# A two-layer hybrid trunk on one core: attention with a different vector split and transposed outputs, an fp32 staggered block preparation, and a delta rule dealt in half steps

## The chip, the core and the metric

The kernel runs on one core of a Trainium2 chip. The core has TensorE (PE in the rows: matmuls, with their weight loads listed apart as PEld), VectorE (DVE), ScalarE (ACT) and GpSimd (POOL), and SyncE (SP), which here does nothing but issue DMAs. Every DMA of this kernel, plain or transposing, is issued by SP, one after the other in program order. The metric is the device time of one execution in microseconds.

## What is computed

Two layers run over 1024 latent tokens and 128 context tokens of width 1024. In each layer three groups of heads read the same normalized input, and their outputs are concatenated, projected and added to the stream:

```python
q = _rope_2d(aq...); k = _rope_2d(ak...)                       # A: attention, 8 query heads, 2 kv heads
o_a = _latent_attention(q, k, v, k_ctx, v_ctx, sink) * silu(ag)   # window of +-128 tokens, plus the context
o_b = _sgu(bu, bv, ...) * silu(bg)                             # B: gated mixing inside 128-token chunks
q_c, k_c, v_c, g, beta = _gdn_features(...)                    # C: gated delta rule, 4 heads, 64-token chunks
a_mat = where(strict, einsum(kb, k) * decay, 0)                # per chunk
t_mat = triangular_solve(a_mat + eye, eye)
def step(state, ...):                                          # chunk after chunk, in both directions
    v_new = u - w @ state
    o     = q_dec @ state + a_qk @ v_new
    state = state * exp(g_last) + k_dec.T @ v_new
x = x + gate * rmsnorm(concat(o_a, o_b, o_c * silu(cg)) @ w_out)
```

## The kernel before, in words

**Tiling.** The tokens are nine tiles of 128: eight latent ones and the context tile, `CTX` = 8. Most operands of matmuls are kept as two f16 halves, a high part and the rest, so that a product takes three f16 matmuls; the delta rule's small 64x64 products are in fp32.

**Two strands in a layer.** `chain()` is the delta rule: the features, then `scan`. `fill()` is everything else that needs the input only: branch B, the gates, and `attention`. `merge` deals them out: the chain yields an estimated cost after each piece, and as much of the fill is emitted as that cost times `FILL` = 0.9 pays for; the tile scheduler then orders each engine's queue by that order of writing. `out_layer` follows alone.

**`scan`.** Ten blocks are prepared first, two of the context and eight of the first pair of heads (about 213 to 302 us of the span in layer 0, 925 to 1005 in layer 1), then comes a triangular solve (`lat_solve`), then `steps(0)`, the 18 steps of the state recurrence for the first pair of heads. The eight blocks of the second pair are prepared inside `steps(0)`, one in every second step. Then a second solve and `steps(1)`. In time: `steps(0)` 380 to 515 and 1080 to 1205 us, `steps(1)` 570 to 690 and 1275 to 1400 us.

**Preparing a block (`prep`, L429).** GpSimd forms the log-decay masks `gt` (L433). The features q and k are fp32; ScalarE, GpSimd and VectorE make f16 halves of them in `PK` (L438 to L443). TensorE transposes the eight pieces (L447) into the PSUM bank of `psw`, ScalarE copies them to `PT` (L449), TensorE forms the products k k and k q (L454) in the same bank's next use, and the sums of the log decays (L459, L460) in the bank of `psv`. ScalarE takes the exponential, `E` (L462), GpSimd multiplies it by beta (L463), VectorE multiplies the products by `E` into `NA` (L465). `psw` and `psv` have one buffer each, and `steps` uses the same two.

**A step of the recurrence (`steps`, L535).** GpSimd scales q and k (`qk` L546, `kd` L548). `pre` turns the scaled q (L556) and forms w (L559) in `psw`. `post` forms v_new (L572, L573) in `psv`, VectorE copies it to `vn` (L575), then come the state's increment (L577), the output (L580, L581) and the new state `S` (L583, L585). The whole of a step is written before the fill gets its turn.

**Attention.** `attention`'s `prep` projects a tile, loads its rotary table `rt` (L889), applies it in `rope_tile` (two multiplies, two half adds: L849 to L854), and turns the f16 halves `ql` into `qT` by a transposing DMA (`turn`, L899). K tiles go the same way first (`rt` at L998). `heads` forms the scores (L921, L922), VectorE adds the mask and takes the maximum (L926), ScalarE makes two exponentials (L928, L929), GpSimd the low half (L931), a transposing DMA makes `PT` (L933). Up to six heads later `weigh` multiplies by V (L947): per key block one matmul of 128 columns (the high half of P with both halves of V) and one of 64 columns. After four heads `normal` forms the denominator (`es` L957, `den` L960 and L961, `rd` L963), scales the gate (L964), adds the two 64-column parts (ScalarE copy L969, VectorE L970) and multiplies (L971). One tile later `finish` transposes the result on TensorE (L977), splits it into f16 halves `OTA` (ScalarE L980, VectorE L981) and writes it to `mix_d` in HBM (L982). `out_layer` reads `mix_d` back.

## Time and profile before

| | us |
|---|---|
| median of 3 runs | 1485.67 (1478.66 to 1486.11) |
| the profiled execution | 1488.63 |
| its span | 1486.8 |
| PE busy, PEld busy | 1312.4 (88%), 1008.0 (68%) |
| DVE busy | 957.6 (64%) |
| ACT busy | 656.4 (44%) |
| POOL busy | 649.5 (44%) |

A busy share is an average over all stages. A windows row gives the same sums for one stretch, with the TensorE clock that was granted there as a part of full speed and the mean busy share of the DMA engines. A groups row puts together all instructions of one line, engine and shape: how many, their summed busy time, the mean duration of one, and the idle time of the engine just before them with what ended it. A matmul's mean duration overlaps with its neighbours', so that the busy time divided by the count is nearer to what one costs in a row of them. A waits row gives how long an engine stood at that line for that releaser, how often, and the longest.

### The profile page before, as it was taken

The numbers are of one execution on the slowest core, as the hardware profiler recorded it, in microseconds if no ns is written. First come the engines' busy times: TensorE is split into PE (matmuls) and PEld (weight loads), VectorE is DVE, ScalarE is ACT, GpSimd is POOL, SyncE is SP. The second block draws the span as 40 slices with busy tenths as digits, with TensorE's granted clock in tenths as the row PEclk, the third lists the DMA queues.
The fourth block names the chain that finished last, engine by engine and source line by source line (L and its number), as shares of the span: only waits on it lengthen the run. The fifth ranks groups of instructions, "written<-read, shape, count | busy, mean of one in ns | idle before, by whom it ended". The sixth has DMA issues, their size and how long they took to land.

```text
span 1486.8 us, 37911 instructions
## 1 busy us (share of the span) xinstructions
PE 1312.4 (88%) x15191; PEld 1008.0 (68%) x15191; DVE 957.6 (64%) x2302; ACT 656.4 (44%) x1483; POOL 649.5 (44%) x890
## 2 busy tenths in 40 slices
PE   6899988799989599979997998879998769997997
PEld 2665566476667487767886655668777658876786
DVE  2865689985565576563547676889586466677333
ACT  2733545523665415642334345442377322665211
POOL 0751246534565325662223433541578514577200
PEclk9999999899999889989998998998899779999999
DMA  9331035727963217683432211332177211677553
GB/s 361 108 84 41 23 98 129 171 74 166 206 165 90 42 52 140 109 228 89 145 113 74 53 36 58 97 71 64 34 134 152 54 39 39 138 122 140 163 177 107
DMA packets 301562, 162.90 MB, mean 110 GB/s; under 512 B 212622, under 2 KB 277938, under 8 KB 301386
## 3 DMA queue, kind: packets, MB, share of 16 engines
q1 hardware_dynamic: 301261, 160.45, 43.8%
q8 instruction: 119, 1.95, 0.6%
q14 instruction: 57, 0.47, 0.1%
q10 hardware_dynamic: 125, 0.04, 0.0%
HBM read 95.78 MB, written 24.28 MB: 81 GB/s over the span
## 4 chain that ended last, share of the span: by engine, by line
PE 42%; DVE 20%; DMA 14%; POOL 10%; issue 9%; ACT 5%; SPq 1%; ACTq 0%; DVEq 0%; POOLq 0%
PE ps L170 11%; PE ps L1052 9%; PE ps L312 6%; DMA PT<-P 4%; DMA mix_d<-oc 3%; DVE sv L502 2%; POOL P L931 2%; DVE sv L500 2%; PE ps L698 2%; PE ps L947 1%; DVE y L319 1%; PE ps L249 1%; DMA wm<-in_w_mod_dram 1%; POOL gt L433 1%; DVE sS L926 1%
## 5 line engine op out<-in xcount | busy, mean ns | idle before, releaser
L170 PEld LDWEIGHTS <-X 128*128 128x128 f16 x3888 | 352.9, 101 | 110.5 <-issue 42.5
L170 PE MATMUL ps<-wg,X 128*128 128x256 f16 x2592 | 331.5, 281 | 11.8 <-DVE wg L161 4.5
L1052 PEld LDWEIGHTS <-OTm 128*128 128x128 f16 x1728 | 169.3, 99 | 24.5 <-DMA OTm<-mix_d 2.5
L931 POOL TENSOR_TENSOR P<-sS,P 128x512 f16<-128x512 f32 (+2 forms) x144 | 152.1, 1060 | 77.1 <-ACT sS L929 75.4
L1052 PE MATMUL ps<-wo,OTm 128*128 128x256 f16 x1296 | 151.0, 276 | 2.1 <-DMA OTm<-mix_d 2.1
L312 PE MATMUL ps<-X,wg 128*128 128x512 f16 (+1 forms) x864 | 146.2, 328 | 1.8 <-ACT wg L160 1.4
L926 DVE CUSTOM_DVE_ANT_0 sS<-ps,am,nsk 128x512 f32<-128x512 f32 (+2 forms) x144 | 95.0, 671 | 52.6 <-POOL P L931 27.7
L928 ACT ACTIVATE P<-sS,nmx 128x512 f16<-128x512 f32 (+2 forms) x144 | 93.6, 660 | 64.2 <-DVE nmx L926 61.9
L170 PE MATMUL ps<-wb,X 128*128 128x256 f16 x864 | 107.9, 289 | 15.2 <-ACT wb L160 13.8
L312 PEld LDWEIGHTS <-wg 128*128 128x128 f16 x864 | 74.0, 99 | 69.1 <-ACT wg L160 1.8
L145 POOL TENSOR_TENSOR rs<-ms,mhalf 128x1 f32<-128x1 f32 x36 | 21.1, 589 | 175.9 <-DVE ms L1061 108.8
L929 ACT ACTIVATE sS<-sS,nmx 128x512 f32<-128x512 f32 (+2 forms) x144 | 94.8, 659 | 3.3
L947 PE MATMUL ps<-Vt,PT 128*128 128x128 f16 (+1 forms) x992 | 69.6, 211 | 26.8 <-DMA PT<-P 23.6
L319 DVE SCALAR_TENSOR_TENSOR y<-zT,cw,y 128x1156 f32<-128x1156 f32 x48 | 68.9, 1439 | 27.5 <-ACT y L317 26.9
L947 PEld LDWEIGHTS <-PT 128*128 128x128 f16 x992 | 51.6, 100 | 45.3 <-DMA PT<-P 30.8
L502 DVE TENSOR_TENSOR sv<-sv 128x31 f32<-128x31 f32 (+15 forms) x186 | 75.0, 403 | 4.3
L500 DVE TENSOR_TENSOR sv<-sv 128x31 f32<-128x31 f32 (+15 forms) x186 | 72.6, 391 | 4.2
L922 PE MATMUL ps<-KT,qT 128*128 128x128 f16 (+2 forms) x272 | 70.1, 273 | 0.0
L921 PE MATMUL ps<-KT,qT 128*128 128x128 f16 (+2 forms) x272 | 61.5, 274 | 8.4 <-DVE nmx L926 6.6
L835 POOL TENSOR_TENSOR th<-th,M 128x256 f32<-128x256 f32 (+1 forms) x20 | 13.5, 679 | 126.4 <-DVE th L834 97.5
L1055 ACT ACTIVATE sq<-ps 128x512 f32<-128x512 f32 x36 | 21.4, 595 | 102.1 <-PE ps L1052 59.1
L288 DVE TENSOR_SCALAR hf<-ps,AB 128x128 f32<-128x128 f32 x117 | 39.7, 402 | 38.9 <-PE ps L281 38.7
(271 smaller groups left out, 2866.8 us busy)
## 6 DMA issues: line engine op xcount, KB each, us to landing
st<-in_w_in_dram SPq DMA_DIRECT2D x40, 512.0 KB
st<-in_w_mod_dram SPq DMA_DIRECT2D x32, 512.0 KB
OTm<-mix_d SPq DMA_DIRECT2D x18, 512.0 KB
wm<-in_w_mod_dram SPq DMA_DIRECT2D x16, 512.0 KB
xt<-in_x_sample_dram SPq DMA_DIRECT2D x16, 512.0 KB
st<-in_w_out_dram SPq DMA_DIRECT2D x16, 512.0 KB
mix_d<-OTA SPq DMA_DIRECT2D x36, 128.0 KB
xs<-xt SPq DMA_DIRECT2D x9, 512.0 KB
```

Of the source, the lines that this page charges most:

```text
L170: T.matmul(ps, X[:, t, k, a, :], wg[:, k, b, c0:c0 + n], start=(i == 0), stop=(i == 23))
L312: T.matmul(ps[:, 0:n], wg[:, k, b, 128 * hg:128 * hg + 128], X[:, t0:t1, k, a, :], start=(i == 0), stop=(i == 23))
L319: V.scalar_tensor_tensor(y, zT[:, tap:tap + 1156], cw[:, tap * 6 + ct:tap * 6 + ct + 1], y, op0=ALU.mult, op1=ALU.add)
L500: V.tensor_tensor(t3, m3[:, 0:m, m:m + 1].to_broadcast([128, m, w]), y3[:, m:m + 1, m:32].to_broadcast([128, m, w]), op=ALU.mult)
L502: V.tensor_tensor(y3[:, 0:m, m:32], y3[:, 0:m, m:32], t3, op=ALU.subtract)
L922: T.matmul(ps[:, cs], qT[:, h, :], Kl[:, kv, ks], start=False, stop=True)
L926: V.tensor_tensor_reduce(sS[:, 0:nk], ps[:, 0:nk], mk, -0.125, nsk[:, hh:hh + 1], ALU.add, ALU.min, accum_out=nmx[:, h:h + 1])
L928: S_.activation(P16[:, 0:nk], sS[:, 0:nk], AF.Exp, bias=nmx[:, h:h + 1], scale=-1.0)
L929: S_.activation(sS[:, 0:nk], sS[:, 0:nk], AF.Exp, bias=nmx[:, h:h + 1], scale=-1.0, accum_out=sm[:, h:h + 1])
L931: G.tensor_tensor(P16[:, nk:2 * nk], sS[:, 0:nk], P16[:, 0:nk], op=ALU.subtract)
L947: T.matmul(pops[:, 128 * h:128 * h + n], PT[:, a * nb + j, :], Vt[:, blist[j], kv].rearrange("p s d -> p (s d)")[:, 0:n], start=(i == 0), ...
L1052: T.matmul(ps[:, 256 * i:256 * i + 256], OTm[:, k, a, :], w[:, k, b, :], start=(n == 0), stop=(n == 23))
```

## The change

Four things change together.

1. **Preparing a block** is split in three functions, staggered by the generator `preps`: in round i the mask and `E` of block i are made, q and k of block i-1 are turned, and the products of block i-2 are formed. Turning is done in fp32, by eight 64x64 matmuls with the identity into one 128x256 PSUM area, which ScalarE copies to `KQ`; the products are four fp32 matmuls of 128 columns. All of `PK`'s casts and copies go. `E` gets four buffers. Ten blocks take twelve rounds (eight take ten).
2. **A step** is dealt in two halves: `post_v` (v_new and `vn`), a yield of 0.5, `post_s` (the rest), a yield of 0.5.
3. **The rotary step** multiplies by a table that now also holds the signed sines for all heads (128x320 instead of 128x128) and reads its input with the halves swapped, so that one full add takes the place of two half adds. `rt` has one buffer instead of two.
4. **Attention's end.** `weigh` uses three 64-column matmuls per key block instead of one of 128 and one of 64 columns, all adding into one 64-column area per head. The add of `es` moves from VectorE to GpSimd. The scaling of `den` and the add of the two parts go; one VectorE instruction multiplies PSUM, a constant and the scaled gate. `finish` goes: ScalarE makes the high half `oh`, GpSimd the low half, a transposing DMA makes `OTA`, and the same `mix_d` write follows it in SP's queue.

```diff
-        def prep(ep, hg, NA, p):
+        def prep_mask(ep, hg, p):
             gt = ep.tile([128, 2, 2, 2, 64], F16, tag="gt", name=nm("gt"))
...
-            PK = ep.tile([128, 4, 2, 128], F16, tag="PK", name=nm("PK"))
-            S_.copy(hl[:, 1], bc(k2, 2, 2))
-            S_.copy(hl[:, 3, :, 0], q2)
-            G.tensor_tensor(hl[:, 2], bc(k2, 2, 2), hl[:, 1], op=ALU.subtract)
-            G.tensor_tensor(hl[:, 3, :, 1], q2, hl[:, 3, :, 0], op=ALU.subtract)
-            V.tensor_copy(hl[:, 0, :, 0], hl[:, 1, :, 0])
-            V.tensor_copy(hl[:, 0, :, 1], hl[:, 2, :, 0])
-            pst = psw(1024, F16)
...
-                    T.transpose(pst[:, (2 * a + h) * 128:(2 * a + h + 1) * 128], PK[:, a, h, :], id16)
-            S_.copy(PT.rearrange("p a h c -> p (a h c)"), pst)
...
-            E = ep.tile([128, 2, 2, 64], F32, tag="E", name=nm("E"))
+            E = ep.tile([128, 2, 2, 64], F32, tag="E", name=nm("E"), bufs=4)
...
+        def prep_turn(ep, hg, p):
+            pst = psw()
+            for i, a in enumerate((1, 0)):
+                for h in range(2):
+                    for hb in (0, 64):
+                        T.matmul(pst[hb:hb + 64, 128 * i + 64 * h:128 * i + 64 * h + 64],
+                                 cqk[hg][hb:hb + 64, p, a, 64 * h:64 * h + 64], ident[hb:hb + 64, hb:hb + 64],
+                                 start=True, stop=True)
+            KQ = ep.tile([128, 2, 2, 64], F32, tag="KQ", name=nm("KQ"))
+            S_.copy(KQ.rearrange("p a h c -> p (a h c)"), pst[:, 0:256])
+            return KQ
+        def prep_mult(hg, NA, p, E, KQ):
+            kkq = psw()
+            for h in range(2):
+                for hb in (0, 64):
+                    T.matmul(kkq[hb:hb + 64, 128 * h:128 * h + 128], KQ[hb:hb + 64, 0, h, :], KQ[hb:hb + 64, :, h, :],
+                             start=True, stop=True)
...
+        def preps(ep, todo):
+            Es, KQs, n = {}, {}, len(todo)
+            for i in range(n + 2):
+                if i < n:
+                    Es[i] = prep_mask(ep, todo[i][0], todo[i][2])
+                if 1 <= i <= n:
+                    KQs[i - 1] = prep_turn(ep, todo[i - 1][0], todo[i - 1][2])
+                if i >= 2:
+                    prep_mult(*todo[i - 2], Es.pop(i - 2), KQs.pop(i - 2))
+                yield 1.0
...
+                half = post_v(r, p, Sc if p == CTX else Sl, cur)
+                yield 0.5
...
-                if i % 2 and i < 16:
-                    prep(gp, 1, NAs[1], i // 2)
-                    cost += share[4]
+                if i in (0, 2) or i % 4 == 3:
+                    next(more, None)
+                    cost += share[4] * 8 / 11
...
-        V.tensor_tensor(a4[:, :, 0, :], a4[:, :, 0, :], u4[:, :, 1, :], op=ALU.add)
-        V.tensor_tensor(a4[:, :, 1, :], a4[:, :, 1, :], u4[:, :, 0, :], op=ALU.add)
+        V.tensor_tensor(u[:, 0:n].rearrange("p (q s f) -> p q s f", s=2, f=16),
+                        src.rearrange("p (q s f) -> p q s f", s=2, f=16)[:, :, ::-1, :],
+                        rt[:, 64:64 + n].rearrange("p (q s f) -> p q s f", s=2, f=16), op=ALU.mult)
+        V.tensor_tensor(a[:, 0:n], a[:, 0:n], u[:, 0:n], op=ALU.add)
...
-                rt = p2.tile([128, 128], F32, tag="rt", name=nm("rt"))
+                rt = p2.tile([128, 320], F32, tag="rt", name=nm("rt"), bufs=1)
...
-                mm = [(0, 0, 128)] + [(j, 1, 64) for j in range(nb)] + [(j, 0, 128) for j in range(1, nb)]
+                mm = [(j, a, s) for j in range(nb) for (a, s) in ((0, 0), (0, 1), (1, 0))]
...
-                V.tensor_tensor(es, sk[:, skv], nmx, op=ALU.add)
+                G.tensor_tensor(es, sk[:, skv], nmx, op=ALU.add)
-                V.tensor_scalar(den, den, 2.0 * WS, None, op0=ALU.mult)
-                S_.copy(oa3, o4[:, :, 1, :])
-                V.tensor_tensor(oa3, oa3, o4[:, :, 0, :], op=ALU.add)
-                V.tensor_tensor(oa, oa, th, op=ALU.mult)
-                    T.transpose(pt[:, 128 * k:128 * k + 128], oa[:, 128 * k:128 * k + 128], ident)
-                S_.copy(OTA[:, :, 0, :], p4)
-                V.tensor_tensor(OTA[:, :, 1, :], p4, OTA[:, :, 0, :], op=ALU.subtract)
+                V.scalar_tensor_tensor(th, pops[:, 0:256], 0.5 * IWS, th, op0=ALU.mult, op1=ALU.mult)
+                S_.copy(oh[:, :, 0, :], oa)
+                G.tensor_tensor(oh[:, :, 1, :], oa, oh[:, :, 0, :], op=ALU.subtract)
+                turn(OTA.rearrange("p k s c -> p (k s) c"), oh.rearrange("p k s c -> p (k s c)"))
                 dma(mix_d[t, :, 2 * kv:2 * kv + 2].rearrange("p k s c -> p (k s c)"), OTA.rearrange("p k s c -> p (k s c)"))
```

**TensorE's queue, late in `steps(0)` of layer 1.** Before, the products of a block (L454, from `PT`) are followed at once by the same block's decay sums (`gt`, `triL`):

```order
L454 MATMUL ps_16363<-PT_16361 64x128
L459 LDWEIGHTS triL_86
L459 MATMUL ps_16372<-gt_16342,triL_86 128x128
L459 LDWEIGHTS triL_86
L459 MATMUL ps_16372<-gt_16342,triL_86 128x128
L460 LDWEIGHTS idb
```

After, at the like place, the products (L460, from `KQ`) stand between the first and the second half of a step (L583 is v_new, L593 the state's increment):

```order
L582 MATMUL ps_15650<-cv_11027,NA_12467 64x64
L583 MATMUL ps_15650<-Sx_15513,qw_15560 64x64
L460 MATMUL ps_15728<-KQ_15538 64x128 x4
L593 MATMUL ps_15650<-vn_15659,kd_15472 64x64 x4
L596 MATMUL ps_15650<-Sx_15513,qw_15560 64x64
```

The decay sums of that block are no longer next to its products; they stand a step earlier in the queue, and what follows here is the next row of the step itself.

**GpSimd's queue, at the same stage.** Before (`PK` are the low halves of k and q, `gt` the masks, `E` the multiply by beta, `ql` the low half of an attention query tile):

```order
L440 TENSOR_TENSOR PK_16345<-cqk_11093,PK_16345 128x256
L441 TENSOR_TENSOR PK_16345<-cqk_11093,PK_16345 128x2x64
L583 TENSOR_TENSOR Sd_16059<-S_15840,eg_11701 128x128
L433 TENSOR_TENSOR gt_16342<-triIc_84,gh_11705 128x256
L433 TENSOR_TENSOR gt_16342<-triIc_84,gl_11706 128x256
L463 TENSOR_TENSOR E_15880<-E_15880,GB_11099 128x256
L897 TENSOR_TENSOR ql_17013<-ra_17004,ql_17013 128x4x64
L546 TENSOR_TENSOR qk_16207<-cqk_11092,eg_11701 128x256
```

After:

```order
L556 TENSOR_TENSOR qk_15849<-cqk_11025,eg_11634 128x256
L433 TENSOR_TENSOR gt_15935<-triIc_84,gh_11638 128x256
L433 TENSOR_TENSOR gt_15935<-triIc_84,gl_11639 128x256
L986 TENSOR_TENSOR oh_16721<-ga_16209,oh_16721 128x2x128
L441 TENSOR_TENSOR E_15526<-E_15526,GB_11032 128x256
L556 TENSOR_TENSOR qk_15892<-cqk_11025,eg_11634 128x256
L599 TENSOR_TENSOR Sd_15699<-Sx_15513,eg_11634 128x128
```

The two `PK` rows are gone, and `E` (L441) belongs to an earlier block than the `gt` rows ahead of it; the subtraction for the attention output (`oh`, L986) is new in the queue.

**SyncE's queue, the second half of attention in layer 0.** Before (`PT` turns a head's weights, `qT` a query tile, `mix_d` writes an output tile):

```order
L982 DMA mix_d<-OTA_8294 128x512
L899 DMA_TRANSPOSE qT_8908<-ql_8905 128x4x128
L933 DMA_TRANSPOSE PT_8619<-P_1341_8614 128x8x128
L933 DMA_TRANSPOSE PT_8653<-P_1349_8648 128x8x128
L933 DMA_TRANSPOSE PT_8741<-P_1371_8736 128x8x128
L933 DMA_TRANSPOSE PT_8769<-P_1377_8764 128x8x128
L982 DMA mix_d<-OTA_8754 128x512
L933 DMA_TRANSPOSE PT_9055<-P_1441_9050 128x8x128
```

After:

```order
L918 DMA_TRANSPOSE qT_9245<-ql_9242 128x4x128
L952 DMA_TRANSPOSE PT_9325<-P_1489_9320 128x8x128
L988 DMA_TRANSPOSE OTA_9351<-oh_9348 128x4x128
L952 DMA_TRANSPOSE PT_9365<-P_1498_9360 128x8x128
L989 DMA mix_d<-OTA_9351 128x512
L952 DMA_TRANSPOSE PT_9391<-P_1503_9386 128x8x128
L988 DMA_TRANSPOSE OTA_9469<-oh_9466 128x4x128
```

Each output tile now has a transposing DMA of its own (`OTA`, from `oh`), and the `mix_d` write that reads its result stands one or two rows behind it in the same queue, ahead of the next heads' `PT`.

## Rows read from the trace of the kernel before

**Rows 1.** First section of the page: busy time, share and instructions by engine.

```profile
PE 1312.4 (88%) x15191; PEld 1008.0 (68%) x15191; DVE 957.6 (64%) x2302; ACT 656.4 (44%) x1483; POOL 649.5 (44%) x890
```

**Rows 2.** Windows view, core 0: span, busy by engine, TensorE clock, DMA share, GB/s.

```profile
235.00:290.00 55.00, 42.58 (x411) 27.82 (x410) 53.87 (x165) 32.40 (x82) 34.73 (x47) 0.94 0.66 156
...
1284.00:1369.00 85.00, 74.84 (x1298) 60.84 (x1296) 58.40 (x180) 56.82 (x147) 64.28 (x90) 1.00 0.72 125
...
1176.00:1209.00 33.00, 22.70 (x460) 19.64 (x457) 12.78 (x39) 10.44 (x21) 11.36 (x23) 0.86 0.06 12
```

**Rows 3.** Groups by line and form, columns as described above: preparing a block.

```profile
L442 DVE COPY PK<-PK 128x128 f16<-128x128 f16 x36 | 12.2, 338 | 7.7 <-ACT PK L438 7.6
...
L443 DVE COPY PK<-PK 128x128 f16<-128x128 f16 x36 | 17.0, 476 | 5.7 <-POOL PK L440 5.7
...
L449 ACT COPY PT<-ps 128x1024 f16<-128x1024 f16 x36 | 36.3, 1007 | 20.2 <-PE ps L447 20.2
...
L447 PE MATMUL ps<-id,PK 128*128 128x128 f16 x288 | 25.5, 238 | 10.8 <-DVE NA L465 8.9 <-DVE NAc L465 1.5 <-DVE PK L443 0.2
...
L454 PE MATMUL ps<-PT 128*64 128x128 f16 x288 | 15.9, 235 | 6.8 <-ACT PT L449 6.7
...
L556 PE MATMUL ps<-ident,qk 64*64 64x64 f32 x576 | 35.6, 238 | 9.3 <-DVE NA L465 7.6 <-ACT qw L562 0.8 <-DVE of L731 0.4
```

**Rows 4.** Timeline (start, length, instruction) 1180 to 1196 us: two preparations.

```profile
1182.48 0.42 PE L454 MATMUL ps<-PT 128*64 128x128 f16 x8 [0.27 <-ACT PT L449]
...
1185.34 0.61 POOL L463 TENSOR_TENSOR E<-E,GB 128x256 f32<-128x256 f32 x1
...
1185.98 0.76 DVE L465 TENSOR_TENSOR NA<-ps,E 128x256 f32<-128x256 f32 x2 [2.06 <-POOL E L463]
...
1192.51 0.42 PE L454 MATMUL ps<-PT 128*64 128x128 f16 x8 [0.26 <-ACT PT L449]
...
1194.61 0.76 DVE L465 TENSOR_TENSOR NA<-ps,E 128x256 f32<-128x256 f32 x2 [1.77 <-POOL E L463]
```

**Rows 5.** Waits of TensorE's matmuls: total us, times, longest.

```profile
PE ps L447 <- DVE NA L465: 8.9, 8, 2.9
...
PE ps L556 <- DVE NA L465: 7.6, 7, 2.2
...
PE ps L577 <- DVE vn L575: 8.5, 5, 3.5
...
PE ps L947 <- DMA PT<-P: 23.6, 25, 2.6
```

**Rows 6.** Groups by line and form: rotary step and attention's closing steps.

```profile
L854 DVE TENSOR_TENSOR ra<-ra,ru 128x128 f32<-128x128 f32 x36 | 14.3, 398 | 0.0
...
L970 DVE TENSOR_TENSOR oa<-oa,ps 128x256 f32<-128x256 f32 x36 | 15.0, 415 | 6.3 <-ACT oa L969 6.0
...
L981 DVE TENSOR_TENSOR OTA<-ps,OTA 128x256 f16<-128x256 f32 x36 | 15.0, 417 | 9.3 <-ACT OTA L980 9.2
...
L897 POOL TENSOR_TENSOR ql<-ra,ql 128x256 f16<-128x256 f32 x36 | 26.2, 729 | 37.8 <-ACT ql L896 37.7
...
L947 PE MATMUL ps<-Vt,PT 128*128 128x64 f16 x496 | 40.0, 196 | 0.0
...
L170 PE MATMUL ps<-wab,X 128*128 128x16 f16 x432 | 12.7, 172 | 6.5 <-ACT X L290 4.1 <-POOL X L291 2.3
```

**Rows 7.** Timeline of SyncE's issuing, 1295 to 1320 us, layer 1.

```profile
1299.74 1.31 SPq L899 DMA_TRANSPOSE qT<-ql  x1
...
1306.74 9.86 SPq L933 DMA_TRANSPOSE PT<-P  x4
```

**Rows 8.** Chain of waits that ended last (start, us, transfer): DMA landings on it.

```profile
450.51 2.73 DMA rt<-in_rope_dram
...
456.69 4.16 DMA qT<-ql
...
1175.79 2.42 DMA qT<-ql
```

More of the change, by code (lines that the diff above doesn't have):

```diff
@@ L624, in steps @@
                     fin = (p, *c_final_norm(l, fp, oacc, p))
[L625 removed]
+                yield 0.5
             if fin is not None:
@@ L1016, in attention @@
                         if i > 0:
-                            yield from heads(p2, prev, *ready.pop(0))
+                            yield from heads(p2, *ready.pop(0))
                             if next(other, None) is not None:
```

91 lines of the change are left out of this document (37 added, 54 removed).

## The prediction

> **What bounds the kernel now.** I read the busy shares first, then the stages, then the single waits. TensorE is busy for 1312.4 of 1486.8 us, VectorE for 957.6, GpSimd for 649.5 [rows 1]. That looks like a kernel bound by matmuls, but a share over the whole span hides that the limits differ by stage. Three stages matter for this change [rows 2]. From 235 to 290 us, where blocks are prepared in layer 0, VectorE is busy for 53.87 of 55 us: there an instruction taken off VectorE can move the end. From 1284 to 1369 us, in `steps(1)` of layer 1 beside the last attention tiles, TensorE has 74.84 of 85 us, VectorE only 58.40, GpSimd 64.28, and the DMA engines are 0.72 busy: VectorE has room there, the others less. From 1176 to 1209 us the fill is used up and the recurrence runs nearly alone: no engine is busy for more than 22.70 of 33 us, so that latency from engine to engine sets the pace. TensorE's waits name the places: 8.9 and 7.6 us for `NA` in preparations, 8.5 us for `vn`, 23.6 us for `PT` [rows 5].
>
> **Part 1, the preparation, in the stretches that run alone.** The single bank of `psw` is held from the products (L454) until VectorE has multiplied them by `E` (L465). In one preparation the products end at 1182.48 + 0.42 = 1182.90 us and VectorE starts at 1185.98, right behind GpSimd's multiply (1185.34, 0.61 long): 3.08 us. In the next one it is 1194.61 - 1192.93 = 1.68 us [rows 4]. In the new order `E` is made two rounds earlier, so that the products find it ready, and the bank is held for the products and the multiply alone. The mean of the two is 2.4 us. Four preparations lie in the stretch of 33 us and three in the like one of layer 0 (499 to 513 us): 7 x 2.4 = 17 us. The lower bound is what TensorE itself is seen to wait for at L556, 7.6 us [rows 5], the upper one 7 x 3.08 = 22. I take **-17**, since the bank also delays work that isn't waiting at L556.
>
> **Part 1, in the preparing stages.** VectorE loses 338 + 476 = 814 ns per block [rows 3], with ten blocks in each layer's stage 16.3 us in all. ScalarE loses the 1007 ns copy of 128x1024 [rows 3] and gets one of a quarter of the elements, which shortens a preparation but not VectorE's list. Against it stands the rotary table: with one buffer, a K tile's table can be fetched only when the tile before has been multiplied, and a fetch lands after 2.73 us on the chain [rows 8]. Eighteen K tiles lie in these stages; if each lost half a microsecond that is 9 us, at no loss nothing, at a full one 18. The rotary add (398 ns twice before, [rows 6], once at full width after) gives back about 0.3 us a tile. I take **-10**: 16 from VectorE and 3 from the adds, less 9. The bounds are -19 and 0, since with the full loss the stage ends where it did.
>
> One rule of the Trainium skill bears on VectorE's copies. The trace shows the copy of L443 at 476 ns and the one of L442, the same shape, at 338 ns [rows 3]; GpSimd's `PK` subtractions run beside the former. The page "SBUF — State Buffer", section "Who interferes with whom", says that a copy which can use both ports, or an operation with two SBUF inputs, excludes GpSimd's SBUF accesses, one of the two blocking until the other is done. By it the removal also frees GpSimd; taking L443's excess of 138 ns as such blocking, the sum over 36 blocks would be 5 us more gain.
>
> **Part 1 on TensorE.** Before, a block cost eight transposes at 25.5/288 = 89 ns and eight products at 15.9/288 = 55 ns, 1.15 us [rows 3]. The new ones are eight fp32 matmuls of 64x64, for which L556 shows 35.6/576 = 62 ns, and four of 128 columns at up to twice that: 0.99 us [rows 3]. The price is between -6 us (36 blocks) and, should the latency of a long fp32 matmul be exposed, 4 x 0.12 x 36 = +17. I take 0, because these lie beside other matmuls except in the stretches counted above.
>
> **Part 2, the half steps, and the eight preparations of each `steps(0)` that have the fill beside them.** TensorE waits 8.5 us in 5 stalls for `vn` [rows 5]: the increment stands behind the copy. With a yield between the halves, a piece of the fill can lie between. I take half of the 8.5 and a little for the issue waits around it, **-5** (bounds -8.5 and 0: some of these stalls lie where the fill is gone). The other nine preparations inside `steps(0)` have fill beside them; I count a quarter of the 2.4 us each, **-5** (bounds 0 and -22).
>
> **Part 3 is in the above.** Beyond the K tiles, 36 query tiles save one half add, 14 us of VectorE [rows 6], in stages where VectorE isn't last: 0, covered by TensorE's matmuls.
>
> **Part 4, attention.** VectorE loses the add of L970 (415 ns), the subtraction of L981 (417) and small ones, so over 1 us for each of 36 tiles [rows 6], in stages where it had room: 0. TensorE gets 496 more matmuls; the columns stay the same (128 + 64 before, three times 64 after). The 16-column matmul at L170 costs 12.7/432 = 29 ns [rows 6], so an extra instruction costs little; the dear end is 40.0/496 = 81 ns each [rows 6], 40 us, less what the halved 128-column ones give back. I take +2, set off by the two transposes per tile that go; the bounds are -10 and +13. What is on the path is SyncE's queue. Each output tile adds a transposing DMA, issued in the 1.31 us that `qT` shows [rows 7]. The `mix_d` write waits for its landing, 2.42 to 4.16 us by `qT` [rows 8], and stands one or two rows behind; while it waits, the next `PT` transposes are not issued. The queue has room: four `PT` issues take 9.86 us because the weights come that slowly [rows 7]. So of about 3 us per tile most lies in gaps. For the 18 tiles of `steps(1)`, where DMA is 0.72 busy, I take half a microsecond each, **+9**; the bounds are 0 and 18 x 2.9 = +52.
>
> A rule of the Trainium skill speaks against this part. The trace shows a 128x256 subtraction into f16 at 729 ns on GpSimd (L897) and 417 ns on VectorE (L981) [rows 6], and the new `oh` moves exactly this from the one to the other. The page "GPSIMD Engine Reference" names VectorE for two-input elementwise work and puts GpSimd at about twice the time; the rows show 1.75 times. By it, 36 x 0.73 = 26 us are added to GpSimd, about what the `PK` subtraction of the same width frees.
>
> **The sum.** -17 - 10 - 5 - 5 + 9 = -28 us. Against the profiled execution, 1488.63 us, that gives 1460.6. That execution is 2.96 us above the median of the runs shown, 1485.67, so the forecast is **1458 us**.
>
> **Rivals.**
>
> *The gain passes through more fully.* VectorE and ScalarE feed the scores' chain, and if TensorE's waits for `PT` (23.6 us) shrink too because the weights come earlier, half of that, 12 us, comes on top, and the K tiles' tables cost nothing (another 9). Then -49, 1437 us. For it: 64% of VectorE's time spread over stages with waits everywhere. Against: in `steps(1)` VectorE isn't last.
>
> *Nothing reaches the end.* The preparing stages could be paced by the K tiles, and the stretches alone by the serial recurrence (v_new, copy, increment, new state), not by the bank. Then part 1 gives only L556's 7.6 us, the rest cancels, and the time is about 1480. This includes that the earlier `E` doesn't do what it says, because the scheduler puts GpSimd's multiply late: in GpSimd's queue `E` stands behind the masks of a later block and behind `oh`.
>
> *SyncE's queue blocks attention (slower).* If every `mix_d` write waits 1.7 us (4.16 landing less two issues of about 1.2), then each of 36 tiles costs 1.3 + 1.7 = 3 us of a queue that also carries `PT`. If in `steps(1)` and the attention beside `steps(0)` half of it reaches TensorE as later `PT`, that is +54, against the gains of 37: +17, 1503 us. The point from which it decides is one microsecond per tile, where 36 us eat the gains. For it: TensorE already waits for `PT` 25 times [rows 5], and DMA is 0.72 busy. Against: the queue mostly waits for weights [rows 7].
>
> **How the numbers follow.** The forecast (1445 to 1472) gets 0.45, the fuller gain 0.18, nothing 0.19, slower 0.18. The range reaches into the fuller gain and over nothing: 1430 to 1490. It leaves out 0.07 below and 0.12 above. A measurement of this kernel can tell about 0.5%, 7.4 us, from no change. Faster (under 1478) takes the first two cases and a fifth of the third: 0.67. Same (to 1493) takes most of the third: 0.16. Slower: 0.17.
>
> **What would show each step.** Right: the wait for `NA` at TensorE's preparing lines falls from 16.5 us to under 4; the stretch alone late in `steps(0)` shortens by about 8 us in each layer; VectorE's busy time falls by about 100 us without the span falling as much; the wait for `PT` stays near 24 us. Wrong: the wait for `PT` rises over 40 us with SyncE standing at the `mix_d` write; K tiles stand over 4 us apart waiting for `rt`; GpSimd's `E` ends after the products in the new order too; or TensorE now waits for `vn` in every step that runs alone.

## The result, and the profile after

The change made the kernel slower: median 1499.55 us of four runs (1493.23 to 1505.71) against 1485.43 us, a ratio of 1.0107 with a 95% interval of 1.0075 to 1.0138, or +14 us. The forecast was 1458 us, -28; the range, up to 1490, didn't hold it. The profiled execution after took 1493.23 us (span 1491.4), the fastest of the four, so its trace shows 4.6 us over the profile of before and not the whole loss.

The page's busy row after, where [rows 1] has the one of before:

```profile
PE 1314.9 (88%) x15903; PEld 1010.5 (68%) x15903; DVE 880.1 (59%) x2032; ACT 608.5 (41%) x1375; POOL 635.8 (43%) x890
```

The vector work went as planned: VectorE 957.6 to 880.1 us, ScalarE 656.4 to 608.5, GpSimd 649.5 to 635.8. TensorE is busy as before, 1314.9 us. Some 139 us of work on three engines went, and the end moved the wrong way.

Where the time went is read by stages, between the first and last new states of the recurrence. The time from 213 us to the last prepared block of layer 0 grew by about 12 us (75.5 to 87.4); the two `steps(0)` became shorter by 6 and 14 us (130.4 to 124.2, 122.8 to 108.6); the two `steps(1)` became longer by 12 and 11 us. All other stages together became 10 us shorter, 6 of them in the stage behind layer 0's preparation (97.5 to 91.4), so that 4.6 us are left. Windows before and then after, of layer 0's preparing stage and of `steps(0)` in layer 0 and 1 (columns: span, busy time of TensorE, its weight loads, VectorE, ScalarE and GpSimd, TensorE clock, DMA share, GB/s):

```profile
213.20:288.70 75.50, 61.62 (x619) 44.15 (x618) 69.80 (x201) 44.05 (x116) 53.30 (x82) 0.96 0.59 140
...
386.20:516.60 130.40, 111.11 (x1717) 84.48 (x1712) 77.78 (x221) 70.21 (x175) 72.43 (x114) 0.97 0.55 118
...
1089.40:1212.20 122.80, 100.28 (x1605) 83.59 (x1603) 72.61 (x205) 68.41 (x165) 73.52 (x112) 0.89 0.48 92
```

```profile
213.00:300.40 87.40, 75.19 (x784) 53.14 (x783) 67.39 (x171) 35.66 (x100) 42.56 (x69) 0.96 0.69 150
...
391.80:516.00 124.20, 109.73 (x1806) 82.97 (x1805) 59.56 (x165) 56.44 (x147) 67.94 (x113) 0.97 0.60 125
...
1098.00:1206.60 108.60, 87.61 (x1672) 73.27 (x1669) 54.73 (x147) 52.62 (x133) 68.95 (x108) 0.93 0.58 104
```

`steps(1)` in layer 0 and 1 after:

```profile
582.50:702.70 120.20, 98.58 (x1528) 80.87 (x1529) 53.55 (x152) 55.20 (x131) 66.51 (x101) 0.83 0.69 147
...
1282.40:1401.80 119.40, 98.88 (x1650) 80.54 (x1645) 60.91 (x172) 60.66 (x150) 76.96 (x111) 0.94 0.77 149
```

And the same two stages before, 583.4 to 692.0 and 1291.7 to 1400.0:

```profile
583.40:692.00 108.60, 91.78 (x1420) 73.94 (x1417) 63.30 (x179) 56.66 (x138) 62.91 (x89) 0.91 0.69 152
...
1291.70:1400.00 108.30, 94.25 (x1552) 77.78 (x1550) 69.91 (x202) 59.72 (x153) 67.61 (x95) 1.00 0.70 144
```

In both, TensorE is busy for longer (98.58 and 98.88 us against 91.78 and 94.25), at a lower granted clock (0.83 and 0.94 against 0.91 and 1.00), and the stage grew by more than that. VectorE, which the change relieved, is busy for 45% and 51% of these stages (58% and 65% before).

Waits of TensorE's matmuls after (total us, times, longest), which answer to [rows 5]; L449 and L566 are the turning and `pre`, L593 the state's increment, L966 the weighing:

```profile
PE ps L966 <- DMA PT<-P: 24.2, 28, 1.9
...
PE ps L593 <- DVE vn L585: 14.8, 11, 3.4
...
PE ps L449 <- DVE NA L463: 3.7, 4, 1.4
...
PE ps L566 <- DVE NA L463: 1.7, 6, 0.4
```

The waits for `NA` fell from 16.5 to 5.4 us; under 4 was named as the sign. The wait for `vn` rose from 8.5 us in 5 stalls to 14.8 in 11. The wait for `PT` stayed, at 24.2.

The chain of waits in the preparing stage of layer 0, its summary by line and two of its pieces after (start, us, what):

```profile
by line: PE ps L170 19.6%; DMA rt<-in_rope_dram 19.0%; DMA st<-in_w_mod_dram 11.1%; PE ps L249 6.7%; DMA OTA<-oh 4.3%; issue 4.1%; DMA st<-in_w_in_dram 3.6%; DVE ra L869 2.5%; POOL P L950 2.3%; PE ps L449 1.9%; DVE ru L870 1.9%; ACT sS L948
...
224.53 3.28 DMA rt<-in_rope_dram
...
233.90 3.28 DMA rt<-in_rope_dram
```

19% of that stage's chain is the fetch of the rotary table; in the like chain of the kernel before, which has two buffers, no such fetch shows. These two tables landed 3.28 us after their issue (160 KB instead of 64), the others on the chain after 2.43 to 4.23 us; the median over all 54 is 2.8 us. VectorE's own waits for a table, before and then after:

```profile
DVE ra L849 <- DMA rt<-in_rope_dram: 2.4, 2, 2.2
```

```profile
DVE ra L869 <- DMA rt<-in_rope_dram: 12.7, 14, 2.9
```

And the end of attention in layer 0, from the same view after, 640 to 672 us (L986 the low half of the output tile, L988 its transposing transfer, L755 the recurrence's output, L1058 the first output projection):

```profile
647.91 1.49 POOL oh L986
...
649.77 0.87 SPq L988
...
650.74 4.01 DMA st<-in_w_out_dram
...
658.06 4.18 DMA mix_d<-oc
...
664.34 1.80 DMA mix_d<-oc
...
666.16 4.55 DMA OTm<-mix_d
```

The second of two weight loads for the output projection stands behind the transposing transfer, which stands behind GpSimd's subtraction; `OTm` is read at 666.16 us, behind two pairs of the recurrence's writes of `mix_d`. SyncE's timeline before had it 10 us earlier, ahead of such a pair (658.39 us):

```profile
648.60 2.46 SPq L158 DMA_DIRECT2D st<-in_w_out_dram  x2
...
655.97 0.81 SPq L1034 DMA_DIRECT2D OTm<-mix_d  x2
```

Until the projection starts, TensorE has nothing but the recurrence. Counting new states up to VectorE's last mask and maximum of scores: before, 10 and 12 of 18 steps were done when attention ended (layer 0 and 1); after, 8 and 10.

### The profile page after: what moved, and what is told of

It is laid out like the page before. It is cut to its first block, busy times and chain, and to the rows that moved or that the text cites. A ratio compares the mean times of both kernels' runs of the same rounds, so it can differ in the third digit from the quotient of the medians.

```text
span 1491.4 us, 38963 instructions
## 1 busy us (share of the span) xinstructions
PE 1314.9 (88%) x15903; PEld 1010.5 (68%) x15903; DVE 880.1 (59%) x2032; ACT 608.5 (41%) x1375; POOL 635.8 (43%) x890
## 4 chain that ended last, share of the span: by engine, by line
PE 46%; DMA 17%; DVE 16%; POOL 8%; issue 6%; ACT 5%; SPq 1%; DVEq 0%; POOLq 0%; ACTq 0%
PE ps L170 12%; PE ps L1058 11%; PE ps L312 6%; DMA PT<-P 4%; POOL P L950 2%; PE ps L249 2%; DMA rt<-in_rope_dram 2%; DMA st<-in_w_mod_dram 2%; DVE sv L510 2%; DVE sv L512 2%; DMA mix_d<-oc 2%; DMA st<-in_w_in_dram 1%; DVE y L319 1%; DVE wg L161 1%; DMA wm<-in_w_mod_dram 1%
## 5 line engine op out<-in xcount | busy, mean ns | idle before, releaser
L170 PEld LDWEIGHTS <-X 128*128 128x128 f16 x3888 | 348.0, 100 | 110.7 <-issue 47.3
L170 PE MATMUL ps<-wg,X 128*128 128x256 f16 x2592 | 327.6, 279 | 14.0 <-DVE wg L161 4.5
L1058 PEld LDWEIGHTS <-OTm 128*128 128x128 f16 x1728 | 170.1, 99 | 31.2 <-DMA OTm<-mix_d 8.1
L1058 PE MATMUL ps<-wo,OTm 128*128 128x256 f16 x1296 | 154.7, 279 | 7.2 <-DMA OTm<-mix_d 7.2
L170 PE MATMUL ps<-wb,X 128*128 128x256 f16 x864 | 104.9, 282 | 16.0 <-ACT wb L160 14.9
L966 PE MATMUL ps<-Vt,PT 128*128 128x64 f16 x1488 | 71.2, 197 | 25.1 <-DMA PT<-P 24.2
L966 PEld LDWEIGHTS <-PT 128*128 128x128 f16 x1488 | 58.7, 100 | 45.8 <-DMA PT<-P 34.1
L512 DVE TENSOR_TENSOR sv<-sv 128x31 f32<-128x31 f32 (+15 forms) x186 | 80.4, 432 | 4.5
L510 DVE TENSOR_TENSOR sv<-sv 128x31 f32<-128x31 f32 (+15 forms) x186 | 73.7, 396 | 4.3
L161 DVE SCALAR_TENSOR_TENSOR wg<-st,wg 128x1024 f16<-128x1024 f32 x44 | 55.9, 1278 | 17.6 <-ACT wg L160 17.6
```

Of the source, the lines that this page charges most:

```text
L161: V.scalar_tensor_tensor(dst[:, 4 * h:4 * h + 4, 1, :cols], s, WS, hi, op0=ALU.mult, op1=ALU.subtract)
L170: T.matmul(ps, X[:, t, k, a, :], wg[:, k, b, c0:c0 + n], start=(i == 0), stop=(i == 23))
L510: V.tensor_tensor(t3, m3[:, 0:m, m:m + 1].to_broadcast([128, m, w]), y3[:, m:m + 1, m:32].to_broadcast([128, m, w]), op=ALU.mult)
L512: V.tensor_tensor(y3[:, 0:m, m:32], y3[:, 0:m, m:32], t3, op=ALU.subtract)
L966: T.matmul(pops[:, 64 * h:64 * h + 64], PT[:, a * nb + j, :], Vt[:, blist[j], kv, s], start=(i == 0), stop=(i == len(mm) - 1))
L1058: T.matmul(ps[:, 256 * i:256 * i + 256], OTm[:, k, a, :], w[:, k, b, :], start=(n == 0), stop=(n == 23))
```

## The experiments

Every median is to be held against the kernel before on the same chip, 1484.2 to 1485.5 us in the five groups of runs. Names of kernels: `undo_x` is the changed kernel without part x, `rope2` the changed kernel with two table buffers, and the later ones start from `rope2`.

**The parts, one undone at a time.** `rope2` is one edit, made at both places:

```diff
-rt = p2.tile([128, 320], F32, tag="rt", name=nm("rt"), bufs=1)
+rt = p2.tile([128, 320], F32, tag="rt", name=nm("rt"))
```

> The changed kernel with one edit: the rotary table's tile has two buffers, as before. Table theory (the preparing stage of layer 0 ended 12 us later because each K tile's table is fetched only after the tile before is multiplied): the stage ends some 10 us earlier and the time falls from 1499.5 to about 1488, ratio to the kernel before about 1.002. Closing theory (the loss is in the output's extra transfer late in each layer's second recurrence, 11 us each): no more than 3 us are gained, about 1497, ratio 1.008. Dealing theory (half steps shift the work): also about 1497.

Measured: 1492.11 us, ratio 1.0052 (1.0031 to 1.0074). The table's one buffer cost 7 us. In its trace the last block of layer 0 is ready at 285.9 us instead of 300.4, and the recurrence behind it takes 16 us longer, so the stage's gain doesn't reach the end one to one.

`undo_attn` takes `weigh`, `normal` and `finish` from the kernel before:

```diff
-                mm = [(j, a, s) for j in range(nb) for (a, s) in ((0, 0), (0, 1), (1, 0))]
+                mm = [(0, 0, 128)] + [(j, 1, 64) for j in range(nb)] + [(j, 0, 128) for j in range(1, nb)]
...
-                turn(OTA.rearrange("p k s c -> p (k s) c"), oh.rearrange("p k s c -> p (k s c)"))
+                    T.transpose(pt[:, 128 * k:128 * k + 128], oa[:, 128 * k:128 * k + 128], ident)
```

> The changed kernel with attention's end as before: 128- and 64-column weighing matmuls, two-part add and multiply on VectorE, transposes on TensorE, no transposing transfer for outputs; the new rotary step with its one buffer stays. Closing theory: the second recurrence of each layer gets its 11 us back, about 1480, ratio 0.997. Table theory: the second recurrences gain little, about 1497, ratio 1.008, since VectorE and ScalarE also get their old work back.

Measured: 1469.48 us, ratio 0.9900 (0.9872 to 0.9928): attention's new end costs 30 us. `steps(1)` of layer 0 takes 106.3 us in this trace and that of layer 1 113.1 (120.2 and 119.4 after), which is the closing theory's place.

`undo_half` deals a step whole:

```diff
-                half = post_v(r, p, Sc if p == CTX else Sl, cur)
-                yield 0.5
...
-                yield 0.5
+                yield 1.0
```

> The changed kernel with each step of the recurrence dealt whole, as before; the preparations are dealt at the same points. Dealing theory (attention now ends one or two steps earlier in the recurrence, which leaves the rest of the second recurrence bare): both second recurrences end 8 to 11 us earlier, about 1480, ratio 0.997. Closing and table theories: within 4 us of 1499, ratio 1.007 to 1.012.

Measured: 1501.98 us, ratio 1.0105 (1.0071 to 1.0138), the same as with half steps. The dealing theory falls in this form; the wait for `vn` is 14.8 us in its trace as well, so it isn't the half steps that raised it, nor did they cure it. It is 8.4 us in 7 stalls in `undo_attn` and 14.1 in `pe_turn` (below), so by these traces it rose with attention's new end, and not with its transposing transfer.

`undo_prep` prepares the blocks by the old `prep`, `if i % 4 == 3 and i < 32: prep(gp, 1, NAs[1], i // 4)` in the half steps.

> The changed kernel with the blocks prepared as before (f16 halves, eight transposes, products and decay sums in one piece, not staggered). All theories hold that the staggering gained, as the first recurrences' bare ends became shorter (6 us in layer 0, 14 in layer 1 in the profile): 1515 to 1520, ratio about 1.02. If the staggering gained nothing at the end, 1499 and ratio 1.01.

Measured: 1521.18 us, ratio 1.0238 (1.0205 to 1.0271): the new preparation is worth 22 us.

`best` joins the good parts: the new preparation, half steps and rotary step with two buffers, with the old end of attention.

> Staggered preparation, half steps and the new rotary step with two buffers of the table; attention's end as before. If the parts add up (16 us under the kernel before without attention's new end, 7 us more from the second buffer), about 1462, ratio 0.985. If the second buffer's gain only shifted work, as rope2's longer first recurrence in layer 0 hints, about 1469, ratio 0.990.

Measured: 1467.05 us, ratio 0.9874 (0.9853 to 0.9895). With the old end, the second buffer brings 2 us (1469.48 without it), within the two intervals, so its 7 us don't add up with the rest.

**What in attention's end costs.** `pe_turn` keeps all of the new end but the transposing transfer; `finish` is back for the one new operand:

```diff
-                oh = p2.tile([128, 2, 2, 128], F16, tag="oh", name=nm("oh"), bufs=1)
-                turn(OTA.rearrange("p k s c -> p (k s) c"), oh.rearrange("p k s c -> p (k s c)"))
+                prev.append((kv, t, th))
...
+                    T.transpose(pt[:, 128 * k:128 * k + 128], oa[:, 128 * k:128 * k + 128], ident)
+                S_.copy(OTA[:, :, 0, :], p4)
+                V.tensor_tensor(OTA[:, :, 1, :], p4, OTA[:, :, 0, :], op=ALU.subtract)
```

> As rope2, but the output tile is turned by TensorE one tile later, as before, instead of by a transposing transfer; the 64-column weighing, the single scaling instruction and the scaled denominator stay new. Transfer theory (the transposing transfer and the write behind it in SyncE's queue cost 20 to 30 us): about 1468, ratio 0.988. Order theory (a cheaper end lets attention run ahead of the recurrence, which is then left bare at its end; in the order of TensorE's queue the last weighing stands after 29 of 36 steps here, 28 in rope2, 30 in the kernel before): only part of it, about 1480, ratio 0.996. Weighing theory (496 more matmuls cost the time): no gain, about 1492.

Measured: 1459.46 us, ratio 0.9811 (0.9780 to 0.9843). 33 us of `rope2`'s time hang on the transposing transfer and what goes with it: the edit also moves the low half from GpSimd to VectorE, adds two TensorE turns per tile and writes a tile later, and it deals anew. The weighing by 64 columns shows no price: TensorE is busy with it for 69.6 us in the kernel before and 71.2 in the changed one. That this kernel is 8 us faster than `best`, which weighs in the old way, says less, since their order differs too.

`late_write` keeps the transfer and issues the write behind it one tile later (`prev.append((mix_d[...], OTA))`, then `dma(*prev.pop())` at head 1 of the next tile).

> As rope2, but the write of an output tile to HBM is issued one tile later, two heads into the next one, so that SyncE's queue never stands at it for the transposing transfer. Transfer theory with the wait as its price: 1475 or less, ratio 0.993. If only the issuing or the order costs: within 4 us of rope2's 1492.

Measured: 1490.42 us, ratio 1.0025 (1.0006 to 1.0044). SyncE stands at that write for 23.4 us in the trace after, and for 26.1 in `rope2`'s. In `late_write` it still stands there, now at two lines, 25.0 us in all (after, then `late_write`):

```profile
SPq L989 <- DMA OTA<-oh: 23.4, 12, 3.6
```

```profile
SPq L969 <- DMA OTA<-oh: 17.8, 11, 3.4
...
SPq L1033 <- DMA OTA<-oh: 7.2, 3, 3.4
```

The edit moved the write and left the wait, so its 2 us, within the two intervals, don't price the wait. The slower rival's mechanism, the write that stands in SyncE's queue, isn't tested by it or by any other run alone. Its sign, a wait for `PT` of over 40 us, didn't show (24.2).

`oh_dve` makes the low half and the sink's add on VectorE (`V.tensor_tensor` for `G.tensor_tensor`, twice).

> As rope2 (1492, outputs turned by the transposing transfer), but the low half of the output tile and the sink's small add are made on VectorE instead of GpSimd. If GpSimd's queue is what the transfer's chain waits in (there `oh` stands ahead of the next heads' low halves and of the recurrence's scalings): 1480 or less, ratio 0.996. If it is not: within 4 us of 1492, ratio 1.002 to 1.008.

Measured: 1494.13 us, ratio 1.0058 (1.0036 to 1.0080): GpSimd's share of the new end isn't the price.

`spare_turn`, `spare_small`, `spare_copy` and `spare_copy3` start from `pe_turn` and add transfers whose result nobody reads, behind the output write:

```diff
+                spare = p2.tile([128, 2, 2, 128], F16, tag="oh", name=nm("spare"), bufs=1)
+                turn(spare..., OTA...)        # spare_turn: 128x512, transposing
+                turn(spare, OTA[:, 0, 0])     # spare_small: 128x128, transposing
+                dma(spare..., OTA...)         # spare_copy: 128x512, plain
+                for i in range(3): dma(spare[:, i], OTA[:, 0, 0])   # spare_copy3: 3 x 128x128, plain
```

> As pe_turn (1459, outputs turned by TensorE), plus one transposing transfer per output tile, of the same size as the one of the change, whose result nobody reads; it is issued behind the output write. If the transposing itself costs (SyncE's issuing, DMA engines that the weights' transposes need too): 1475 to 1492, ratio 0.993 to 1.005. If only what depends on the transfer costs (the order, the chain to the output): 1459 to 1465, ratio about 0.983.

> As spare_turn (1480; pe_turn without any spare transfer 1459), but the spare transposing transfer has 128 columns instead of 512: one quarter of the data, one instruction of SyncE all the same. If SyncE's issuing is the price: still about 1478, ratio 0.995. If the data in the DMA engines is: about 1464, ratio 0.986.

> As spare_turn, but the spare transfer is a plain copy of the same 128 KB instead of a transposing one. If SyncE's issue time is the price (a plain transfer shows 0.5 us there, a transposing one 1.2): about 1467, ratio 0.988. If the amount of data is: about 1478, ratio 0.995. If only transposing traffic disturbs the weights' transposes: 1460, ratio 0.983.

> As pe_turn (1459), plus three plain spare copies of 32 KB per output tile, together 1.5 us of SyncE's issuing, more than the 1.2 us of one transposing transfer. If SyncE's issue time as such is the price: 1475 to 1485, ratio 0.994 to 1.000, as spare_small (1476). If it is that the transfer transposes: 1457 to 1464, ratio 0.984, as spare_copy (1460).

| kernel | median us | over `pe_turn` | ratio to before (95%) |
|---|---|---|---|
| pe_turn | 1459.46 | | 0.9811 (0.9780 to 0.9843) |
| spare_turn | 1479.65 | +20.2 | 0.9969 (0.9947 to 0.9990) |
| spare_small | 1476.26 | +16.8 | 0.9946 (0.9923 to 0.9969) |
| spare_copy | 1459.76 | +0.3 | 0.9829 (0.9806 to 0.9853) |
| spare_copy3 | 1466.08 | +6.6 | 0.9876 (0.9858 to 0.9895) |

36 transposing transfers that nobody reads cost 17 to 20 us; 36 plain copies of the same 128 KB cost nothing that shows, and three plain copies a tile, about 1.7 us of SyncE's issuing against 1.2 for one transposing transfer, cost 6.6 us. By the medians alone neither the data nor SyncE's issuing time is the price. SyncE's rows of `spare_turn`, `spare_copy` and `spare_copy3` (ns held, min/median/max):

```profile
L999 SPq DMA_TRANSPOSE spare<-OTA x36: 1188/1204/2424, 283.4 to 1371.0; - x36
```

```profile
L999 SPq DMA_DIRECT2D spare<-OTA x36: 476/505/1363, 284.8 to 1342.1; - x36
```

```profile
L1000 SPq DMA_DIRECT2D spare<-OTA x108: 464/564/1842, 281.2 to 1353.8; - x108
```

But not all of the 17 to 20 us is paid where a spare transfer is issued. From the last new state of layer 0 to the preparation of layer 1 SyncE issues no transposing transfer in any of these kernels, and yet this border takes 9 and 11 us longer with the transposing spare than in `pe_turn` (`pe_turn`, `spare_turn`, `spare_small`, `spare_copy`):

```profile
692.10:916.70 224.60, 214.34 (x1918) 161.45 (x1915) 141.30 (x261) 93.86 (x161) 73.30 (x71) 0.98 0.29 87
```

```profile
698.00:933.60 235.60, 213.87 (x1868) 158.91 (x1868) 140.15 (x255) 91.52 (x155) 73.01 (x70) 0.95 0.27 78
```

```profile
686.00:919.60 233.60, 214.24 (x1890) 159.66 (x1888) 142.04 (x259) 92.05 (x156) 73.38 (x69) 0.96 0.27 81
```

```profile
684.40:911.30 226.90, 217.38 (x1914) 163.74 (x1914) 141.07 (x260) 93.19 (x160) 73.19 (x71) 0.96 0.29 86
```

TensorE is busy there for the same 214 us in the first three; its queue is in another order (in `spare_turn` 98 matmuls of `wab`, L170, stand ahead of the next turns at L281, in `pe_turn` 2). Outside the border the profiled executions of `spare_turn`, `spare_small`, `spare_copy` and `spare_copy3` are 18, 9, -1 and 7 us over `pe_turn`'s; the first is the slowest of its kernel's twelve runs, 9.6 us over their median, so that 8 is nearer to it. There, about a quarter of a microsecond for each transposing transfer (an estimate from one trace of each kernel), the three plain copies cost as much. So the runs show that the plain copy was free and the transposing transfer was not, with a quarter of the data or with all; whether that is the transposing, the longer issue or the order isn't shown. How it gets to TensorE isn't shown either: TensorE waits for `PT` for 30.1 us in `spare_turn`, but for 31.4 in `spare_copy3`. `rope2`, at 233.6 us, has the slow border as well, so 9 of its 33 us over `pe_turn` lie there.

**The dealing.** `fill86` is `rope2` with `FILL = 0.86`.

> As rope2, but FILL is 0.86 instead of 0.9, so that less of the other strand is dealt out per piece of the chain; in TensorE's queue the last weighing of layer 0 then stands after 31 of 36 steps (28 in rope2, 30 in the kernel before), that of layer 1 after 68 of 72 (66 in rope2, 68 before). Order theory: the bare ends of the second recurrences shrink by about 10 us each, 1474, ratio 0.992. Transfer theory: no gain, 1488 to 1496.

Measured: 1462.70 us, ratio 0.9842 (0.9820 to 0.9864): 29 us gained with the transposing transfer in place. For a while that looked like the order theory's proof. Three controls followed: the old kernel with 0.86, `pe_turn` with 0.86, and `pe_turn` with 0.84.

> The kernel before with FILL at 0.86 and nothing else, a control of fill86: is its gain (30 us under rope2) a cure of the change's order, or would the dealing have helped the old kernel as much? Order theory (the change made attention run ahead, 0.86 puts it back): in the old kernel the last weighing moves only from step 30 to 31 in layer 0 and not at all in layer 1, so within 6 us of 1485, ratio 0.996 to 1.004. If 0.86 is simply the better setting: about 1465, ratio 0.986.

> The two cures at once: outputs turned by TensorE (1459 alone) and FILL at 0.86 (1463 alone, with the transposing transfer). Order theory (both take away the same loss): no sum, 1450 to 1462, ratio about 0.980; attention may now stand too late, after 33 of 36 and 70 of 72 steps. Transfer theory (the transfer has a price of its own, and 0.86 gains elsewhere): the gains add up, about 1432, ratio 0.965.

> As pe_turn86 (1437) with FILL 0.84: the last weighing of layer 1 stands behind the last step (72 of 72; 70 with 0.86). Order theory: attention now outlasts the recurrence, and what was gained is lost in part, 1440 to 1460, ratio 0.970 to 0.983. If less dealing is simply better: under 1435.

Measured: 1502.20 us (1.0108, 1.0078 to 1.0137), 1436.85 us (0.9685, 0.9657 to 0.9713) and 1456.62 us (0.9809, 0.9782 to 0.9835). The same number costs the old kernel 18 us and brings `pe_turn` 23; two hundredths further 20 of the 23 are gone again. `pe_turn86` is the fastest kernel of this study, 48 us under the one before. Its `steps(1)` stages, 569.9 to 679.1 and 1244.5 to 1350.0 us:

```profile
569.90:679.10 109.20, 95.95 (x1666) 79.96 (x1663) 67.46 (x182) 61.09 (x152) 71.05 (x104) 1.00 0.76 161
...
1244.50:1350.00 105.50, 96.03 (x1659) 79.29 (x1655) 61.60 (x179) 60.48 (x153) 71.33 (x106) 0.95 0.75 148
```

They take 109.2 and 105.5 us, 11 and 14 less than after, at a clock of 1.00 and 0.95; attention ends there after 12 and 14 of 18 steps. The order theory held that the two cures share one loss. They added up instead (33 and 29 alone, 55 together, from `rope2`), so at that point it fell.

`share_prep` (with the transposing transfer) and `pe_share` (without) scale only the planner's costs of a preparation by 0.87, `FILL` at 0.9:

```diff
-SHARE = ((1.08, 5.56, 1.88, 2.27, 5.93, 1.0, 2.13), (1.39, 4.8, 2.03, 2.16, 2.49, 1.87, 1.7))
+SHARE = ((1.08, 4.84, 1.88, 2.27, 5.16, 1.0, 2.13), (1.39, 4.18, 2.03, 2.16, 2.17, 1.87, 1.7))
```

> As rope2 (1492, outputs turned by the transposing transfer) with FILL at 0.9, but the planner's costs of preparing a block, made for the old preparation, are scaled by 0.87. If fill86 (1463) gained because the preparation is now shorter than the planner takes it for, and too much of the other strand was dealt out beside it: about 1468, ratio 0.989. If it gained through the dealing elsewhere: 1485 to 1495, ratio 1.000 to 1.007.

> The same scaled costs with the outputs turned by TensorE (1459 with the old costs, 1437 with FILL 0.86). If the preparation's costs are what was out of date: about 1438, ratio 0.969. If not: 1455 to 1462, ratio 0.982.

Measured: 1469.81 us (0.9906, 0.9879 to 0.9933) and 1458.02 us (0.9828, 0.9804 to 0.9852). With the transfer 22 us are gained, without it 1. A stale cost explains the first, not the second. What the dealing does stays open beyond this: the same instructions in another order are 18 to 29 us apart, by no rule that these runs show.

The transposing transfer, though, costs under each of the three dealings: 1492.11 against 1459.46, 1462.70 against 1436.85, 1469.81 against 1458.02, or 33, 26 and 12 us. In the last two pairs the border between the layers takes the same time with and without it (within 2 us), so nothing of the 26 and 12 lies there.

## Why the prediction was wrong, point by point

- **Preparation in the stretches that run alone (-17), and part of the preparing stages.** Right in direction and mechanism, too large in the sum: -17, -16 and -5 were counted on for the preparation, and undone it is worth 22 us. Part of the excess is a reading: in the trace before, the stretch of 499 to 513 us has the products of one preparation, not of three, and the one of 1176 to 1209 those of three, not four, so that the -17 would be -10 (4 x 2.4). In the preparing stages, with two table buffers, `rope2` gains 4 and 7 us (75.5 to 71.9, 81.8 to 74.7) of the 19 counted on. The mechanism is as put: in the timeline after, a block's products end at 1167.45 us and VectorE starts at 1167.50, where it was 3.08 and 1.68 us before [rows 4]. The two `steps(0)` shortened by 6 and 14 us; about 8 each were forecast.

```profile
1166.80 0.65 PE L460 MATMUL ps<-KQ 64*64 64x128 f32 x8
...
1167.50 0.76 DVE L463 TENSOR_TENSOR NA<-ps,E 128x256 f32<-128x256 f32 x2 [0.33 <-PE ps L460]
```

- **The table's one buffer (+9 inside the -10).** Right in mechanism and nearly in size at the end: 7 us by `rope2`. In the stages themselves it costs more than the bound of 18: 15.5 us in layer 0 (87.4 to 71.9) and 4.5 in layer 1 (79.2 to 74.7). In the profiled execution the stage of layer 0 grew by 12 us where the far bound was 0. The rule weighed there, on VectorE and GpSimd excluding each other (the Trainium skill, "SBUF — State Buffer", "Who interferes with whom") isn't tested by any run: none moves that work alone. The 138 ns taken for it rest for two thirds on one copy of 3579 ns; the medians at L443 and L442 are 402 and 308 ns.
- **Half steps (-5).** Wrong: no gain. The step that failed is that a yield between the halves puts other work there; with whole and with half steps TensorE waits 14.8 us for `vn`, and what brings it back to 8.4 is attention's old end.
- **TensorE (0).** Right in sum, 1312.4 to 1314.9 us busy, by terms that offset each other. Turning and products in fp32 take (26.9 + 24.7) / 36 = 1.43 us per block (L449, L460) where 1.15 stood and 0.99 was forecast, 10 us more in all; the forecast divided by the rows' count, which has two records for each fp32 matmul (x576 for 288). The two turns per output tile that went give back 15.3 us, and the weighing grew by 1.6.
- **Attention's end (+9, bounds 0 and +52).** The step that failed: it measures 30 us (`undo_attn`), in the place that was named, SyncE's queue, or at least by the transfer that was put into it. Two things in it were wrong. It counted only the 18 tiles of `steps(1)`, at half a microsecond. In the profiled executions of `rope2` and `pe_turn` the two `steps(1)` are 5 and 6 us apart, but the two `steps(0)` 8 and 11, and the border between the layers 9. And it gave the transposing transfer no price of its own beside its issuing and the write that waits for it, while transposing transfers that nobody reads cost 17 to 20 us, 9 to 11 of them at that border. The row behind the estimate, SyncE's `PT` issues spread over 9.86 us [rows 7], says that the queue has gaps; it doesn't say that a transposing transfer put into a gap is free for the next one. By which way the transfer reaches TensorE stays open. The rule that speaks against the move to GpSimd (the Trainium skill, "GPSIMD Engine Reference", 4.1 "Engine selection") doesn't come out at about twice the time here: the same `oh` takes 760 ns on GpSimd and 701 on VectorE (after, then `oh_dve`). The 417 ns of the forecast were of a subtraction that reads PSUM, while `oh` has both inputs in SBUF. The move cost nothing at the end (`oh_dve`).

```profile
L986 POOL TENSOR_TENSOR oh<-ga,oh 128x256 f16<-128x256 f32 x36 | 27.4, 760 | 18.0 <-ACT oh L985 16.1 <-issue 1.2 <-POOL kd L558 0.7
```

```profile
L986 DVE TENSOR_TENSOR oh<-ga,oh 128x256 f16<-128x256 f32 x36 | 25.2, 701 | 4.0 <-ACT oh L985 3.8
```

- **What was left out: the order.** The second step that failed is a term at nothing. Nothing in the sum had a term for the planner, whose costs were made for the old durations. A kernel with fewer vector instructions is dealt and ordered differently, and the runs above show 18 to 29 us for order alone, in either sign. That is as large as the whole forecast.
- **The sum.** Measured one part at a time: -21.6 for the preparation, +7.4 for the buffer, +30.1 for attention's end and -2.4 for the half steps (not beyond its interval) make +13.5; +14.1 was measured. That they add up so well is partly luck: the buffer is worth 7.4 us beside the new end and 2.4 beside the old one. The slower rival had the right place, attention in the recurrence's company by way of the transfer in SyncE's queue; whether its mechanism, the waiting write, has a part in the 30 us stays open. It was given 0.18. The forecast's 1458 us is, by chance of other terms too, what `pe_turn` takes: the change without its transposing transfer and with both buffers.

## What to carry to other kernels

Price a DMA that transposes by adding one that nobody reads, before moving work from an idle-looking engine to the queue: here 36 copies of the same size were free and 36 transposing ones cost 20 us. Then look where in the trace the loss lies: half of it stood in a stage without any such transfer, where TensorE's queue was in another order. When a change alters the durations that a planner deals by, tune the planner again before judging the change: with both table buffers the same edit was +0.5% or -1.6% by one constant, and without its transposing transfer -1.9% or -3.2%. And undo a mixed change part by part; four runs showed that it held -22 and +30 at once.

## What the runs showed of the hardware that had not been expected

- **A transposing DMA that nobody reads was not free where a plain one was.** SyncE is held for 1.20 us by it (median) and for 0.51 by a plain copy of the same 128 KB (rows above), 25 us more over 36. At the end 36 of them cost 20.2 us against 0.3, of which 9 to 11 go with the order at the border of the layers; the rest is no more than three plain copies a tile cost. From issue to landing it takes a median of 4.0 us, the plain copy 2.6 (`spare_turn`, `spare_copy`):

```profile
DMA to landing us min/median/max: 2.4/4.0/4.9
```

```profile
DMA to landing us min/median/max: 2.0/2.6/4.1
```

The Trainium skill ("Advanced Engine Details and Errata", "X-Bar Transpose (TRN2)") calls transposing DMAs as fast as regular ones; for this size and this queue the rows of issue and landing say otherwise.
- **The granted clock adds to the price of an idle stretch.** At the border of the layers, in the windows of 10 us each of `pe_turn` and then of `rope2` (span, busy by engine, clock, DMA share, GB/s):

```profile
782.00:792.00 10.00, 7.25 (x106) 6.10 (x107) 8.18 (x16) 5.89 (x7) 3.77 (x4) 0.66 0.49 160
...
792.00:802.00 10.00, 9.66 (x194) 8.96 (x192) 3.58 (x11) 1.60 (x3) 3.56 (x2) 1.00 0.15 42
```

```profile
788.00:798.00 10.00, 1.72 (x38) 1.43 (x39) 8.69 (x17) 5.46 (x10) 3.67 (x4) 0.69 0.48 149
...
798.00:808.00 10.00, 10.00 (x183) 9.14 (x180) 5.40 (x15) 4.39 (x5) 3.06 (x3) 0.63 0.17 64
```

In `pe_turn` TensorE is busy for 7.25 of 10 us, and the next 10 us have the full clock. In `rope2` it is busy for 1.72, and the next 10 us, in which it is never idle, run at 0.63 of full speed; by an estimate from that mean, some three quarters of them ((1 - 0.63) / 0.5) at 1.2 GHz instead of 2.4. The order of TensorE's queue differs at the two borders as well. The mean clock of whole executions moves with the times: 0.952 to 0.956 in `pe_turn86`, 0.932 to 0.948 in the kernel before, 0.912 to 0.927 in `undo_prep`. How much of each difference is the clock's and how much the idle time's own, these runs don't separate.
